# Half of the last pooled output projection moved among the first score tiles of an encoder block

## The chip, the cores and the metric

The kernel runs on one core of a Trainium2 chip. The metric is the device time of one execution in microseconds (us), and the median of several executions counts. The engines are PE (TensorE, the matmuls, with PEld for its weight loads), DVE (VectorE), ACT (ScalarE), POOL (GpSimd) and SP (SyncE, which here only issues DMAs).

## What is computed

One layer of a streaming encoder over 2048 tokens of width 1024: a mixer with two branches, a cross attention to 256 memory tokens and a SwiGLU. The change lies where the mixer's two branches meet:

```python
xn = rmsnorm(h, g_mix[l])
z = jnp.einsum('bsd,dc->bsc', xn, w_in[l])
# q, k, v, p_in, f_logit are column ranges of z; q, k are normalised by head
fox = forgetting_attention(q, k, v, f_logit.transpose(0, 2, 1))   # 8 heads of 64, causal
pool = multiscale_pool(p_in, w_pool[l], pool_scale[l])            # 4 groups of 128 channels
h = h + jnp.einsum('bsc,cd->bsd', jnp.concatenate([fox, pool], axis=-1), w_out[l])
```

`multiscale_pool` takes for group g the trailing mean over 2, 4, 8 or 16 frames less the frame itself, then a 128 x 128 map and a scale per channel. The kernel folds that map into the lower half of `w_out`. The forgetting attention has scores q.k plus a difference of cumulated log gates, a causal mask and a softmax.

## The kernel before

Every float32 operand of a matmul is split into a high and a low part; a product takes three matmuls (`mm3`, lines 69 to 71: high x high, high x low, low x high). Scores take two (line 846).

**Pool stage** (lines 631 to 751). Tokens go in 8 blocks of 256 (two row blocks of 128). Iteration n of a loop of ten projects block n to its pooled channels (`project_p`, tile `zp`), forms the windows on VectorE (`windows`, tile `mixed`), splits `mixed` of block n-1 into `mxh` and `mxl` (`mixed_parts`: a cast on ScalarE, a subtraction on VectorE), and multiplies block n-2 with the folded weights `wop` (`out_pool`). For each row block and each half of 512 columns `out_pool` issues 4 groups x 3 matmuls into a bank `oo`; VectorE adds the bank to the rows of x (`xr`, line 702, "the sum"), and the finished row goes to `h1d` in DRAM (line 703, by GpSimd's queue, for the last block by SP's). In this stage only PE's order is that of the code; a scheduler orders the other engines by their readiness.

**Score stage** (from line 789). Per head and block of 512 rows b there are four rows of 128 (q), and each needs b+1 tiles of up to 512 columns (`score_items`). A tile is two matmuls into one of three banks `sps`, then one reduction on VectorE (line 848), which adds the gates `cb` or, on the diagonal, the masked gates `cm`, and keeps the minimum. `cm` is made by GpSimd (`masked_row`, line 824), three rows ahead, in three small tiles. ScalarE takes the exponential (line 859). 22 score tiles (`LEAD`) go first; then the loop alternates between value steps (`value_items`: transposes `tp`, line 56, their split, the product `acc` with the values, line 922) and score tiles. `later(n, fn)` puts an instruction n steps further into the code. Here PE, DVE, ACT and POOL run in the order of the code.

**Places in SBUF.** A head's `qs`, `kh`, `kl`, `cb` are four tiles of 128 x 2048 in the pool `hpa` (even heads) or `hpb` (odd heads). Head 0 is loaded during the pool stage; `hpb` is opened only behind that stage, and head 1 is loaded into it by SP when head 0 reaches b = 1 (`load_head`, line 619). Before, the `pt` pool holds what the pool stage needs: `xr` (4 row buffers, used in turn, first by the raw weights `wr`), the windows' tiles, `mxh` and `mxl`.

Of the kernel before, what the change touches and what calls it, by code (L numbers as in the profile page):

```python
# [41 lines left out]
def block_kernel(ctx: ExitStack, tc: tile.TileContext, x, xT, memT, cols, rows, w_qkvf, w_p, w_pool, w_out,  # L42
# [9 lines left out]
    def f(ap):  # L52
        return ap.bitcast(F32)
# [141 lines left out]
    with ExitStack() as c0:  # L195
# [167 lines left out]
        with ExitStack() as c1:  # L363
# [129 lines left out]
            def cumulated():  # L493

                HN = H * NT
                cp = lambda n: pt.tile([P, HN], F32, name=n)
                utri, e, mn = cp("utri"), cp("fe"), cp("fmin")
# [9 lines left out]
                yield  # L507
                tots = pt.tile([P, H, NT], F32, name="tots")
                car = pt.tile([P, H, NT], F32, name="car")
                tot = tpp.tile([P, HN], F32, tag="ss", name="tot", bufs=1)  # L510
# [79 lines left out]
            wq_ = opened(xstack, "wo_pool", side="right")  # L590
            pt = opened(xstack, "pt", side="right")
            xt = x_load(1)
            for k in range(NPRE, KD):
# [9 lines left out]
            for g in range(NG):  # L603

                wop_raw.append(pt.tile([P, D], F32, tag="xr", name="wr", bufs=4))
                sp.dma_start(wop_raw[g][:], w_out[FOXW + g * P:FOXW + (g + 1) * P, :])
# [11 lines left out]

    def load_head(h, pl, *after):
        qs, kh, kl = (slab(n, pl, F32R) for n in range(3))  # L620
        cb = slab(3, pl)
        loads = []
        own = slice(h % 2 * DH, (h % 2 + 1) * DH)
        for a in range(2):
            to = slice(a * DH, (a + 1) * DH)
            loads += [(f(qs[to, :]), qkT[0][a][h // 2, own]), (f(kh[to, :]), qkT[1][0][h // 2, own]),
                      (f(kl[to, :]), qkT[1][1][h // 2, own])]
        for to, src in (*loads, (cb[:], cdr[h].partition_broadcast(P))):
            needs(sp.dma_start(to, src), *after)
        return qs, kh, kl, cb  # L630


    with xstack:
# [25 lines left out]
        def windows(b, pT):  # L659
            cur = pT  # L660
            mixed = pt.tile([P, NG, B], F32, tag="mixed", name="mixed")
            for st in range(NG):
                sh = 1 << st
                lead = 2 * sh - 1
                nx = pt.tile([P, NG, HIS + B], F32, tag=f"s{st % 2}", name=f"s{st}")
                dve.tensor_tensor(out=nx[:, st:, lead:], in0=cur[:, st:, lead:],
# [10 lines left out]

        def mixed_parts(mixed):
            mxh = pt.tile([P, NG, B], F32R, tag="mxh", name="mxh", bufs=2)
            mxl = pt.tile([P, NG, B], F32R, tag="mxl", name="mxl", bufs=2)  # L680
            act.copy(mxh[:], mixed[:])
            sub_hi(mxl[:], mixed[:], mxh[:])
            return mxh, mxl
# [3 lines left out]
        def out_pool(b, mxh, mxl):  # L687
            for j in range(2):
                i = 2 * b + j
                ts = slice(j * P, (j + 1) * P)  # L690
                if b < NB - 1:
                    xr = pt.tile([P, D], F32, tag="xr", name="xr", bufs=4)[:]
                    sp.dma_start(xr, x[i * P:(i + 1) * P, :])
                else:
                    xr = x_last[:, j]
                for a in range(2):
                    ps = tpp.tile([P, 512], F32, tag="tp", name="oo", bufs=3)
                    for g in range(NG):
                        mm3(ps[:], (mxh[:, g, ts], mxl[:, g, ts]), (wop[g, a][0][:], wop[g, a][1][:]),
                            g == 0, g == NG - 1)  # L700
                    as_ = slice(a * 512, (a + 1) * 512)
                    summed[:] = [dve.tensor_tensor(out=xr[:, as_], in0=ps[:], in1=xr[:, as_], op=ALU.add)]
                (pool if b < NB - 1 else sp).dma_start(h1d[i][:], xr)

        with in_order():
            mixed, mxs, wop = {}, {}, {}
            for n in range(NB + 2):
# [23 lines left out]
                if n == NB:  # L731
                    lstack.close()
                    hp = opened(hps, "hp")

                    x_last = hp.tile([P, 2, D], F32, tag="v", name="xr", bufs=2)
                    sp.dma_start(x_last[:], x[(NT - 2) * P:, :].rearrange("(j p) c -> p j c", p=P))
                    v0 = load_values(0)
                if n == 2:
                    fold_w_pool()
                if n - 2 >= 0:  # L740
                    out_pool(n - 2, *mxs.pop(n - 2))
                if 0 <= n - 1 < NB:
                    mxs[n - 1] = mixed_parts(mixed.pop(n - 1))
# [22 lines left out]

    FOX = 6
    first_row = []

    TWO, LATER = 3, 7  # L770

    last_parts = []
    hpb = opened(hps, "hpb")
    wof, wq, cats = {}, {}, {}
# [13 lines left out]
    with ExitStack() as c0:  # L788
# [204 lines left out]
        def all_scores():  # L993
            for un in units:
                h, b = un["u"]
                if b == 1 and h + 1 < H:
                    heads[h + 1] = load_head(h + 1, (hpa, hpb)[(h + 1) % 2])
                elif b == 1:
                    load_w_of()
# [12 lines left out]
        def all_values():  # L1012
            for un in units:
                yield from value_items(un)

        def first_fox():
# [13 lines left out]
        with in_order(EN.DVE, EN.Activation, EN.Pool):  # L1030
# [3 lines left out]
            lead, more = 0, True  # L1034
            alone, fox = 0, first_fox()
            while True:
                if more and lead < LEAD:
                    n = next(sg, None)
                    more = n is not None
                    lead += more  # L1040
                else:
                    n = next(vg, None)
# [896 lines left out]
```

## Time and profile before

| | |
|---|---|
| median of 3 executions | 2478.37 us (2477.61 to 2479.3) |
| the profiled execution | 2477.7 us |
| its span, first to last instruction | 2476.0 us |
| PE busy in the span | 2461.1 us (99%) |
| DVE, ACT, POOL busy | 1753.4, 1227.4, 678.7 us |
| pool stage, last matmul issued | 502.27 us after the span's start |

All positions below are microseconds from the span's start. In the trace's rows a matmul of 512 columns is shown with 0.39 us, but its successor may start before it ends; distances between starts are what tells how densely PE issues. "Idle before" an instruction comes in brackets at the end of its row with the one that ended it. In a table of windows each engine has its busy time, with the number of its instructions in brackets.

### The profile page before, as it was taken

The page shows a single profiled execution, that of the slowest core. Times are in us where ns is not written, and L with a number is a line of the kernel's source. Part 1 is how long each engine was busy: PE and PEld are TensorE (multiplying, and loading weights), DVE is VectorE, ACT ScalarE, POOL GpSimd, SP SyncE. Part 2 cuts the span into 40 slices and gives each one's busy share as a digit, 9 for nine tenths or more (in the row PEclk, how much of TensorE's full clock was granted, in tenths as well). Part 3 has the DMA queues.
Part 4 walks back from the last instruction along what each step waited for, and adds up shares of the span by engine and source line. Part 5 has one row for each costly group of instructions (what it writes and reads, how often), then busy time and mean ns, then how long its engine had stood idle before and what let it go on. Part 6 is the DMA issues. An engine that isn't in the chain of part 4 may idle for free.

```text
span 2476.0 us, 37877 instructions
## 1 busy us (share of the span) xinstructions
PE 2461.1 (99%) x13295; PEld 2119.4 (86%) x13295; DVE 1753.4 (71%) x3354; ACT 1227.4 (50%) x2360; POOL 678.7 (27%) x939
## 2 busy tenths in 40 slices
PE   9999999999999999999999999999999999999999
PEld 8999989878888788888888888888888888888887
DVE  7444485489999845456998888867687777775554
ACT  7434441079999845445544444345454333334443
POOL 2233300045555523343133323310002222222000
PEclk9999999999999999999999999999999999999999
DMA  8665566476776543233555554567873233335766
GB/s 296 212 196 168 169 200 175 167 194 155 174 162 157 147 151 107 109 109 128 200 204 196 183 195 167 193 225 254 269 254 107 111 132 115 115 124 179 233 208 209
DMA packets 236991, 436.38 MB, mean 176 GB/s; under 512 B 26416, under 2 KB 124720, under 8 KB 225968
## 3 DMA queue, kind: packets, MB, share of 16 engines
q1 hardware_dynamic: 207536, 339.30, 44.1%
q0 software_dynamic: 29120, 94.39, 10.2%
q8 instruction: 105, 1.72, 0.3%
q14 instruction: 86, 0.70, 0.1%
q10 hardware_dynamic: 144, 0.26, 0.0%
HBM read 295.33 MB, written 133.56 MB: 173 GB/s over the span
## 4 chain that ended last, share of the span: by engine, by line
PE 79%; DMA 3%; DVE 2%; ACT 1%; issue 1%; SPq 0%; POOL 0%; DVEq 0%; ACTq 0%; POOLq 0%
PE bk L69 16%; PE bk L70 15%; PE bk L71 15%; PE acc L922 5%; PE sps L846 5%; PE tp L56 4%; PE mmps L69 3%; PE mmps L70 3%; PE mmps L71 3%; DMA draw<-wt 1%; PE oo L71 1%; PE oo L69 1%; PE oo L70 1%; PE zp L71 1%; PE zp L69 1%; PE zp L70 1%
## 5 line engine op out<-in xcount | busy, mean ns | idle before, releaser
L64 DVE TENSOR_TENSOR ww<-draw,ww 128x512 fp32r<-128x512 f32 x308 | 205.1, 701 | 137.3 <-ACT ww L184 137.0
L184 ACT CAST ww<-draw 128x512 fp32r<-128x512 f32 x308 | 180.7, 620 | 199.8 <-PE bk L71 123.9
L70 PE MATMUL bk<-ww,ww 128*128 128x512 f32 x619 | 240.5, 389 | 1.4 <-DVE ww L64 1.4
L71 PE MATMUL bk<-ww,ww 128*128 128x512 f32 x619 | 240.2, 388 | 0.0
L69 PE MATMUL bk<-ww,ww 128*128 128x512 f32 x619 | 240.2, 388 | 0.0
L64 DVE TENSOR_TENSOR pl<-tp,ph 128x512 fp32r<-128x512 f32 (+3 forms) x298 | 177.0, 596 | 10.3 <-ACT ph L955 10.1
L69 PE MATMUL zps<-wh,xhi 128*128 128x384 f32 (+1 forms) x512 | 174.1, 340 | 0.0
L64 DVE TENSOR_TENSOR ww<-graw,ww 128x512 fp32r<-128x512 f32 x198 | 151.6, 768 | 31.2 <-ACT ww L1166 28.8
L71 PE MATMUL zps<-wh,xl 128*128 128x384 f32 (+1 forms) x512 | 172.0, 336 | 0.0
L70 PE MATMUL zps<-wl,xhi 128*128 128x384 f32 (+1 forms) x512 | 171.9, 336 | 0.0
L1166 ACT CAST ww<-graw 128x512 fp32r<-128x512 f32 x176 | 108.3, 617 | 120.9 <-PE bk L71 112.3
L955 ACT CAST ph<-tp 128x512 fp32r<-128x512 f32 (+3 forms) x298 | 152.5, 529 | 23.5 <-PE tp L56 21.6
L70 PEld LDWEIGHTS bk<-ww,ww 128*128 128x128 f32 x619 | 116.2, 188 | 26.4 <-DVE ww L64 2.6
L69 PE MATMUL bk<-kl,ww 128*128 128x512 f32 x352 | 137.8, 392 | 0.0
L69 PE MATMUL bk<-qs,ww 128*128 128x512 f32 x352 | 137.2, 390 | 0.0
L70 PE MATMUL bk<-kh,ww 128*128 128x512 f32 x352 | 137.2, 390 | 0.0
L71 PE MATMUL bk<-kl,ww 128*128 128x512 f32 x352 | 137.1, 389 | 0.0
L70 PE MATMUL bk<-cb,ww 128*128 128x512 f32 x352 | 137.0, 389 | 0.0
L71 PE MATMUL bk<-qs,ww 128*128 128x512 f32 x352 | 137.0, 389 | 0.0
L69 PEld LDWEIGHTS bk<-ww,ww 128*128 128x128 f32 x619 | 116.2, 188 | 24.0
L71 PEld LDWEIGHTS bk<-ww,ww 128*128 128x128 f32 x619 | 116.2, 188 | 23.9
L846 PE MATMUL sps<-kh,qs 128*128 128x512 f32 (+2 forms) x320 | 124.6, 390 | 0.8 <-DVE mx L848 0.4
(666 smaller groups left out, 7210.5 us busy)
## 6 DMA issues: line engine op xcount, KB each, us to landing
graw<-in_w_gu_dram SPq DMA_DIRECT2D x44, 1024.0 KB, 4.8
draw<-wt SPq DMA_DIRECT2D x88, 256.0 KB, 4.9
draw<-in_w_down_dram SPq DMA_DIRECT2D x66, 256.0 KB, 4.4
xl<-in_xT_dram SPq DMA_DIRECT2D x64, 256.0 KB, 5.9
wdr<-in_w_down_dram SPq DMA_DIRECT2D x44, 256.0 KB, 3.6
wt<-wdr POOLq DMA_DIRECT2D x22, 512.0 KB, 3.1
xrow<-in_x_dram SPq DMA_DIRECT2D x16, 512.0 KB, 5.0
vd<-cb SPq DMA_DIRECT2D x16, 512.0 KB, 3.6
```

What stands on the lines that cost most here:

```text
L56: return pe.transpose(out.bitcast(F32R), src, identr[:])
L64: (eng or dve).tensor_tensor(out=lo, in0=src, in1=f(hi), op=ALU.subtract)
L69: pe.matmul(ps, lhsT=sh, rhs=mh, start=first, stop=False, skip_group_check=goes_on)
L70: pe.matmul(ps, lhsT=sh, rhs=ml, start=False, stop=False, skip_group_check=goes_on)
L71: pe.matmul(ps, lhsT=sl, rhs=mh, start=False, stop=last, skip_group_check=goes_on)
L184: act.copy(hi, raw)
L846: pe.matmul(ps[:, :w], lhsT=qs[:, i * P:(i + 1) * P], rhs=kk[:, cs], start=(a == 0), stop=(a == 1))
L922: pe.matmul(acc[:m, q0 * P:], lhsT=v[:, j, :m], rhs=(pl if low else ph)[:, q0 * P:], start=state["n"] == 1, stop=state["n"] == 2 * nk)
L955: act.copy(ph[:, sl], tp[:, sl])
L1166: w["cast"] = act.copy(quad(hi), v)
```

## The change

The last block's `out_pool` keeps only its left 512 columns. The right 512 columns of its two row blocks (24 matmuls, 2 sums) become a generator `last_pool`, of which one group of three matmuls is issued behind each of the score tiles 4, 6, ... 18 (table `POOLED`). It writes into the banks `acc` that the first value steps use afterwards, and the sums come in two steps later.

For this the operands must outlive the pool stage. `hpb` is opened at n = 8, in place of a new pool `pta` (the `xr` rows, some windows' tiles and the tiles of `cumulated`), which is closed there. `mixed` of the last block is split at once, into `hpb`'s `qs`; the right half of `wop` is copied by eight DMAs of SP, inside SBUF, into `hpb`'s `kh` and `kl`. Rows 12 and 13 of x are loaded and written in halves through the three small tiles that `cm` uses later. The row buffers `xr` are taken in another turn, (i + 2) mod 4. Since `hpb` is in use until score tile 20, the six loads of head 1's `qs`, `kh`, `kl` follow tile 22 and are issued by GpSimd; only its `cb` stays with SP.

```diff
@@ load_head @@
-    def load_head(h, pl, *after):
+    def load_head(h, pl, *after, by=None):
...
-        for to, src in (*loads, (cb[:], cdr[h].partition_broadcast(P))):
+        for to, src in (*(loads if by is None else ()), (cb[:], cdr[h].partition_broadcast(P))):
             needs(sp.dma_start(to, src), *after)
+        if by is not None:
+            by.extend(loads)
@@ out_pool @@
-                if b < NB - 1:
-                    xr = pt.tile([P, D], F32, tag="xr", name="xr", bufs=4)[:]
-                    sp.dma_start(xr, x[i * P:(i + 1) * P, :])
+                if b < NB - 2:
+                    xr_row = pta.tile([P, D], F32, tag=f"xr{(i + 2) % 4}", name="xr", bufs=1)[:]
+                    sp.dma_start(xr_row, x[i * P:(i + 1) * P, :])
+                    xr = [xr_row[:, :512], xr_row[:, 512:]]
+                elif b == NB - 2:
+                    xr = [hp.tile([P, 512], F32, tag="cm", name="xr", bufs=3)[:] for _ in range(2)]
+                    for a in range(2):
+                        sp.dma_start(xr[a], x[i * P:(i + 1) * P, a * 512:(a + 1) * 512])
                 else:
-                    xr = x_last[:, j]
-                for a in range(2):
+                    xr = [x_last[:, j, :512]]
+                for a in range(len(xr)):
...
-                (pool if b < NB - 1 else sp).dma_start(h1d[i][:], xr)
+                    if b == NB - 2:
+                        pool.dma_start(h1d[i][:, a * 512:(a + 1) * 512], xr[a])
+                if b < NB - 2:
+                    pool.dma_start(h1d[i][:], xr_row)
@@ the loop of the pool stage, n == NB @@
                     v0 = load_values(0)
+                    ptas.close()
+                    hpb = opened(hps, "hpb")
+                    last_mx = mixed_parts(mixed.pop(n - 1), slab(0, hpb, F32R)[:])
+                    mxs[n - 1] = last_mx
+                    late_w = [slab(c, hpb, F32R)[:] for c in (1, 2)]
+                    for c in range(2):
+                        for g in range(NG):
+                            sp.dma_start(f(late_w[c][:, g * 512:(g + 1) * 512]), f(wop[g, 1][c][:]))
...
-                if 0 <= n - 1 < NB:
+                if 0 <= n - 1 < NB - 1:
                     mxs[n - 1] = mixed_parts(mixed.pop(n - 1))
@@ the score stage @@
+    POOLED = (4, 6, 8, 10, 12, 14, 16, 18, 20)
...
-                if b == 1 and h + 1 < H:
+                if b == 1 and 0 < h and h + 1 < H:
                     heads[h + 1] = load_head(h + 1, (hpa, hpb)[(h + 1) % 2])
...
+        def last_pool():
+
+            for j in range(2):
+                ps = aps.tile([P, 512], F32, tag="acc", name="oo", bufs=2)
+                ts = slice(j * P, (j + 1) * P)
+                for g in range(NG):
+                    mm3(ps[:], tuple(t_[:, g, ts] for t_ in last_mx), tuple(t_[:, g * 512:(g + 1) * 512] for t_ in late_w),
+                        g == 0, g == NG - 1)
+                    yield
+
+                def summed_(j=j, ps=ps):
+                    xr = x_last[:, j]
+                    dve.tensor_tensor(out=xr[:, 512:], in0=ps[:], in1=xr[:, 512:], op=ALU.add)
+                    sp.dma_start(h1d[NT - 2 + j][:], xr)
+
+                later(2, summed_)
...
                     lead += more
+                    scored += 1
+                    if scored in POOLED:
+                        next(lastp, None)
+                    if scored == POOLED[-1] + 2:
+                        own = []
+                        heads[1] = load_head(1, hpb, by=own)
+                        for m, a_ in enumerate(own):
+                            later(m + 1, lambda a_=a_: pool.dma_start(*a_))
```

On PE, at the first score tiles (`sps`, operands `qs`, `kh`, `kl` of head 0), before the change:

```order
L846 MATMUL sps<-kh,qs 128x384
L846 MATMUL sps<-kl,qs 128x384
L846 MATMUL sps<-kh,qs 128x512
L846 MATMUL sps<-kl,qs 128x512
L846 MATMUL sps<-kh,qs 128x512
```

and after it, where `oo` is the moved product and its `kh`, `kl`, `qs` are `hpb`'s:

```order
L868 MATMUL sps<-kh,qs 128x384
L868 MATMUL sps<-kl,qs 128x384
L868 MATMUL sps<-kh,qs 128x512
L868 MATMUL sps<-kl,qs 128x512
L69 MATMUL oo<-kh,qs 128x512
L70 MATMUL oo<-kl,qs 128x512
L71 MATMUL oo<-kh,qs 128x512
L868 MATMUL sps<-kh,qs 128x512
```

Three matmuls of the pooled projection now stand between the fourth and the fifth score tile, and so on to tile 18.

On GpSimd, from the last rows of the pool stage on (`h1d` is a finished row, `cm` a mask), before:

```order
L703 DMA h1d_121<-xr 128x1024
L824 AFFINE_SELECT cm<-cb 128x128
L824 AFFINE_SELECT cm<-cb 128x256
L824 AFFINE_SELECT cm<-cb 128x384
L831 MEMSET l 128x8
L703 DMA h1d_122<-xr 128x1024
```

and after it:

```order
L715 DMA h1d_124<-xr 128x512 x2
L715 DMA h1d_125<-xr 128x512
L846 AFFINE_SELECT cm<-cb 128x128
L846 AFFINE_SELECT cm<-cb 128x256
L715 DMA h1d_125<-xr 128x512
L846 AFFINE_SELECT cm<-cb 128x384
```

The first three masks have moved behind row 12 and among the halves of row 13. Further on, at score tile 22, GpSimd has after the change:

```order
L846 AFFINE_SELECT cm<-cb 128x256
L1088 DMA qs<-qkT0h 64x2048
L895 TENSOR_TENSOR li<-l 128x4
L1088 DMA kh<-qkT1h 64x2048
L1088 DMA kl<-qkT1l 64x2048
L1088 DMA qs<-qkT0l 64x2048
L1088 DMA kh<-qkT1h 64x2048
L1088 DMA kl<-qkT1l 64x2048
L846 AFFINE_SELECT cm<-cb 128x384
```

Head 1's six loads are new there, between two masks of head 0's last rows.

## Rows read from the trace of the kernel before

**Rows 1.** The page: table of engines (busy us, instructions) and granted clock by slice.
```profile
PE 2461.1 (99%) x13295; PEld 2119.4 (86%) x13295; DVE 1753.4 (71%) x3354; ACT 1227.4 (50%) x2360; POOL 678.7 (27%) x939
...
PEclk9999999999999999999999999999999999999999
```

**Rows 2.** Timeline of PE: start, duration, instruction, idle before it, releaser.
```profile
497.06 0.39 PE L69 MATMUL oo<-wop00h,mxh 128*128 128x512 f32 x1
...
502.51 0.22 PE L846 MATMUL sps<-kh,qs 128*128 128x128 f32 x1
...
503.45 0.45 PE L846 MATMUL sps<-kh,qs 128*128 128x384 f32 x1 [0.32 <-DVE xr L702]
...
514.26 0.46 PE L56 MATMUL tp<-identr,s0g 128*128 128x128 f32 x4
...
535.36 0.29 PE L846 MATMUL sps<-kh,qs 128*128 128x128 f32 x1
```

**Rows 3.** Windows: length, busy time of PE, PEld, DVE, ACT, POOL, clock, DMA.
```profile
502.50:514.26 11.76, 10.97 (x45) 6.71 (x44) 11.22 (x48) 9.14 (x19) 4.74 (x13) 1.00 0.88 206
...
514.26:520.33 6.07, 5.66 (x37) 4.29 (x36) 6.07 (x26) 5.57 (x16) 1.12 (x4) 1.00 1.02 248
520.33:527.63 7.30, 6.80 (x42) 4.92 (x42) 5.79 (x18) 7.08 (x17) 3.92 (x6) 1.00 0.57 221
527.63:535.36 7.73, 7.73 (x55) 6.54 (x55) 7.28 (x24) 6.97 (x14) 3.68 (x5) 1.00 0.37 88
```

**Rows 4.** Waits from 502 to 560: total us, times, longest.
```profile
PEld sps L846 <- DVE mx L848: 4.0, 13, 0.4
```

**Rows 5.** Timeline of VectorE: sums of rows 12 and 13, the last sum, score tiles.
```profile
483.66 0.69 DVE L702 TENSOR_TENSOR xr<-oo,xr 128x512 f32<-128x512 f32 x1 [0.59 <-PE oo L71]
...
491.82 0.69 DVE L702 TENSOR_TENSOR xr<-oo,xr 128x512 f32<-128x512 f32 x1 [2.03 <-PE oo L71]
...
502.71 0.69 DVE L702 TENSOR_TENSOR xr<-oo,xr 128x512 f32<-128x512 f32 x1 [2.04 <-PE oo L71]
...
504.22 0.56 DVE L848 CUSTOM_DVE_ANT_0 s0g<-sps,cm 128x384 f32<-128x384 f32 x1 [0.27 <-PE sps L846]
...
504.70 0.69 DVE L848 CUSTOM_DVE_ANT_0 s0g<-sps,cm 128x512 f32<-128x512 f32 x1
...
505.31 0.69 DVE L848 CUSTOM_DVE_ANT_0 s1g<-sps,cb 128x512 f32<-128x512 f32 x1
```

**Rows 6.** DMA issues in short windows: count, KB each, us from issue to landing.
```profile
h1d<-xr POOLq DMA_DIRECT2D x1, 512.0 KB, 2.9
...
xr<-in_x_dram SPq DMA_DIRECT2D x2, 512.0 KB, 4.1
...
qs<-qkT0h SPq DMA_DIRECT2D x1, 512.0 KB, 5.1
...
kl<-qkT1l SPq DMA_DIRECT2D x1, 512.0 KB, 14.2
...
v<-vd SPq DMA_DIRECT2D x1, 1024.0 KB, 6.9
```

**Rows 7.** Timelines of SP, ScalarE and PE in the early pool stage.
```profile
353.40 0.38 SPq L156 DMA_DIRECT2D xl<-in_xT_dram  x1
...
358.47 0.62 ACT L165 CAST xhi<-xl 128x512 fp32r<-128x512 f32 x1 [1.49 <-DMA xl<-in_xT_dram]
...
361.63 0.39 PE L69 MATMUL oo<-wop31h,mxh 128*128 128x512 f32 x1
```

**Rows 8.** Timeline of GpSimd: the mask ahead of head 1's first load.
```profile
514.98 0.40 POOL L824 TENSOR_SCALAR_AFFINE_SELECT cm<-cb 128x256 f32<-128x256 f32 x1 [1.59 <-DVE mx L848]
```

**Rows 9.** Groups of GpSimd's instructions: busy us, mean ns of one, idle before.
```profile
L906 POOL DMA_DIRECT2D catT<-fo x28 | 24.0, 858 | 12.1 <-DMA catT<-fo 12.1
```

**Rows 10.** SP's queue: first and last of head 2's six loads.
```profile
538.97 0.54 SPq L629 DMA_DIRECT2D qs<-qkT0h  x1
...
542.11 0.59 SPq L629 DMA_DIRECT2D kl<-qkT1l  x1
```

More of the change, by code (lines that the diff above doesn't have):

```diff
@@ L495, in cumulated @@
                 HN = H * NT
-                cp = lambda n: pt.tile([P, HN], F32, name=n)
+                cp = lambda n: pta.tile([P, HN], F32, name=n)
                 utri, e, mn = cp("utri"), cp("fe"), cp("fmin")
@@ L507, in cumulated @@
                 yield
-                tots = pt.tile([P, H, NT], F32, name="tots")
-                car = pt.tile([P, H, NT], F32, name="car")
+                tots = pta.tile([P, H, NT], F32, name="tots")
+                car = pta.tile([P, H, NT], F32, name="car")
                 tot = tpp.tile([P, HN], F32, tag="ss", name="tot", bufs=1)
@@ L591, in block_kernel @@
             pt = opened(xstack, "pt", side="right")
+            ptas = ExitStack()
+            pta = opened(ptas, "pta", side="right")
             xt = x_load(1)
@@ L603, in block_kernel @@
             for g in range(NG):
-                wop_raw.append(pt.tile([P, D], F32, tag="xr", name="wr", bufs=4))
+                wop_raw.append(pta.tile([P, D], F32, tag=f"xr{g}", name="wr", bufs=1))
                 sp.dma_start(wop_raw[g][:], w_out[FOXW + g * P:FOXW + (g + 1) * P, :])
@@ L664, in windows @@
                 lead = 2 * sh - 1
-                nx = pt.tile([P, NG, HIS + B], F32, tag=f"s{st % 2}", name=f"s{st}")
+                nx = (pt if st % 2 else pta).tile([P, NG, HIS + B], F32, tag=f"s{st % 2}", name=f"s{st}")
                 dve.tensor_tensor(out=nx[:, st:, lead:], in0=cur[:, st:, lead:],
@@ L676, in windows, with mixed_parts @@
             return mixed
[L678 to L682, printed above, removed]
+        def mixed_parts(mixed, place=None):
+            if place is None:
+                mxh = pt.tile([P, NG, B], F32R, tag="mxh", name="mxh", bufs=2)[:]
+                mxl = pt.tile([P, NG, B], F32R, tag="mxl", name="mxl", bufs=2)[:]
+            else:
+                mxh, mxl = (place[:, c * NG * B:(c + 1) * NG * B].rearrange("p (g t) -> p g t", g=NG) for c in range(2))
+            act.copy(mxh, mixed[:])
+            sub_hi(mxl, mixed[:], mxh)
             return mxh, mxl
@@ L700, in out_pool @@
                             g == 0, g == NG - 1)
-                    as_ = slice(a * 512, (a + 1) * 512)
-                    summed[:] = [dve.tensor_tensor(out=xr[:, as_], in0=ps[:], in1=xr[:, as_], op=ALU.add)]
-                (pool if b < NB - 1 else sp).dma_start(h1d[i][:], xr)
+                    summed[:] = [dve.tensor_tensor(out=xr[a], in0=ps[:], in1=xr[a], op=ALU.add)]
+                    if b == NB - 2:
+                        pool.dma_start(h1d[i][:, a * 512:(a + 1) * 512], xr[a])
+                if b < NB - 2:
+                    pool.dma_start(h1d[i][:], xr_row)
         with in_order():
@@ L772, in block_kernel @@
     last_parts = []
-    hpb = opened(hps, "hpb")
     wof, wq, cats = {}, {}, {}
@@ L995, in all_scores @@
                 h, b = un["u"]
-                if b == 1 and h + 1 < H:
+                if b == 1 and 0 < h and h + 1 < H:
                     heads[h + 1] = load_head(h + 1, (hpa, hpb)[(h + 1) % 2])
-                elif b == 1:
+                elif b == 1 and h > 0:
                     load_w_of()
@@ L1034, in block_kernel @@
             lead, more = 0, True
-            alone, fox = 0, first_fox()
+            alone, fox, lastp = 0, first_fox(), last_pool()
+            scored = 0
             while True:
```

## The prediction

> **What bounds the kernel now.** [...] In the last row block of the pool stage the first matmul of 24 starts at 497.06 and the first score matmul follows at 502.51 [rows 2]: 24 matmuls of 512 columns in 5.45 us, 0.227 each. Nothing waits there.
>
> Then come the score tiles. The first 22 stand alone on PE, until the first transpose at 514.26 [rows 2]: 11.75 us. They hold 44 matmuls with 17,920 columns in all (1,280 + 3,328 + 4,352 for the first, second and third block of rows, each done twice); at 0.227 per 512 that is 7.95. So 3.8 us of PE are lost. The windows and the waits say to whom: VectorE is busy for 11.22 of 11.76 us, and PE's weight loads wait for its reductions 13 times, 4.0 us in all [rows 3, 4]. A tile of 512 keeps VectorE from 504.70 to 505.31, 0.61 [rows 5], and PE for 0.45, and PE has three banks to run ahead in. After that VectorE is full for 6.07 us more and ScalarE for 7.08 of 7.30, where PE's idle is 0.41 and 0.50 [rows 3]; from 527.63 PE has none.
>
> **The moved matmuls.** 24 of the last 48 matmuls of the pool stage (right half of the columns, both row blocks) go behind score tiles 4, 6, ... 18, three at a time. The score tiles then start 5.45 sooner, at 497.06. PE has 7.95 + 5.45 = 13.4 us to issue in the 22 tiles, VectorE 11.2 plus two sums of 0.6 each (a row is 0.69 long, and the next begins some 0.08 before its end, as the tiles of 512 do [rows 5]) = 12.4. So PE becomes the longer one, and the two are nearly even. If PE never waited, tile 22 would end 13.4 after 497.06 and 3.8 us would be won, all that was lost. Some waits stay: the 0.32 before tile 3 [rows 2], since no group stands ahead of tile 4, and what two engines with 13.4 and 12.4 us of work and three banks between them lose at unequal tiles and where a sum holds VectorE for 0.6, which I put at 0.5. I take 3.8 - 0.8 = **3.0**, with 1.8 (PE pays both sums in full, a further 1.2) and 3.8 as ends.
>
> Behind tile 22 two things pull apart. The sums add 1.2 us to VectorE just ahead of a stretch where it is full; but ScalarE, which is full after that, has had 1 to 2 us longer for the exponentials of these tiles. From the rows the place can give back at most PE's idle, 0.41 + 0.50 = 0.9, and lose half a sum, 0.6. I take 0, nearest to the even sum of both.
>
> **The operand made sooner.** The split of the last block's mixed columns on ScalarE and VectorE now stands ahead of the last-but-one block's projection. VectorE does only a sum every 2.7 us there (483.66 to 491.82, three steps [rows 5]), and PE reads the operand a whole block later. 0, and its bounds with it.
>
> **Copies and halves on SP's queue.** Eight copies inside SBUF (2 MB) wait for the writes of rows 10 and 11, which GpSimd's queue lands 2.9 us after issue [rows 6]. The load of the second half of row 13 stands behind them on SP and waits for the first write of row 12. From the rows: row 12's first sum ends at 484.35 [rows 5], landed at 487.3, then a load that takes 4.1 at most (twice the size, [rows 6]) is there at 491.4; VectorE wants it at 491.82 [rows 5]. Were it 1 us late, VectorE's sum moves, and PE has a free bank: 0. The score masks now use the three small tiles of rows 12 and 13. The second mask waits for row 13's first write (sum at 489.1, landed by 493.2) and the last write stands behind it on GpSimd, so it lands by 496.6 and the third mask is there at about 497.1. VectorE wants it 5.45 before 504.22 [rows 5], at 498.8. I take 0; at 1 us beyond the cover VectorE and then PE pay 1.
>
> **Early row loads.** On SP the loads of rows 0 and 1 now wait for later weight splits, and those of rows 2 and 3 pass three loads of x. There ScalarE waited 1.49 us, until 358.47, for a load of x issued at 353.40; a weight cast stands behind it, which with VectorE's half of the split is done some 1.9 later (two casts of 0.62 [rows 7], a subtraction of 0.69 like the sums) at 360.4; PE reads that weight from 361.63 and its low part a matmul later, at 361.86 [rows 7]. So 1.5 of cover. SP's block moves about 3 us of transfers later, which then flow without gaps. Ends 0 and 1.5; I take 0, since the last of these loads isn't moved itself.
>
> **Head 1 by GpSimd's queue.** Six loads of 512 KB leave SP and follow tile 22 on GpSimd. Ahead of them there stands the mask that was issued at 514.98 [rows 8]; with 3.0 won that is 512.0. Behind them wait the masks of the last two rows of head 0, wanted some 12 us later. What such loads take: head 2's six, issued on SP from 538.97 to 542.11, land 5.1 (the first) and 14.2 us (the last) after their issue, 17.3 from the first issue to the last byte [rows 6, 10]. That gives 529.3. Head 1's first score matmul is at 535.36 [rows 2], with 3.0 won at 532.4: 3 us of margin, and this is the cover. Into it falls the load of head 1's values on SP, 6.9 us by itself [rows 6]; if all of it went ahead, the keys would come at 536.2, 3.8 too late, and PE pays that in full, because its matmuls are in order. Two queues share, so I take 0 and keep 3.8 as the other end.
>
> GpSimd spends 0.86 us on an issue amid busy VectorE [rows 9]; six make 5.2, inside the 17.3. [...]
>
> **Sum.** 3.0 + 0 = 3.0 us, about 0.12%. The profiled execution took 2477.7 (span 2476.0 and 1.7 around it), 0.7 under the median 2478.37. Its successor: 2474.7; against the median **2475.4**. The ends of the first two terms together: 3.8 + 0.9 = 4.7 won and 1.8 - 0.6 = 1.2 won; with the mask or the early loads at their bad end (1 and 1.5) next to nothing is won.
>
> **Rivals.**
> 1. Nearly all 5.45 comes back: ScalarE's chain, not VectorE's, sets the way to 527, and starts 5.4 sooner. For it: ScalarE is full to 527 [rows 3]. Against: VectorE is full before that and gains only 3. 4.0 to 5.4 won: 2473.0 to 2474.4.
> 2. The change only moves the time: the sums and the late mask hold VectorE, which was the bound, and what PE saves ahead it waits among the tiles. For it: VectorE's 11.22 of 11.76. Against: 1.2 us of sums is less than 5.45 of matmuls. 0 to 1 won: 2477.4 to 2478.4.
> 3. Head 1 lands 1 to 4 us late because values and keys share the DMA engines. For it: 17.3 us for the 3 MB of keys alone [rows 6, 10], 20.4 from 512.0 to 532.4 for keys and values. 0 to 2 won: 2476.4 to 2478.4.
> [...]
>
> **How the numbers follow.** The forecast has 0.55, rival 1 0.20, rival 2 0.08, rival 3 0.12, rival 4 0.05. A measurement of this kernel can tell 0.2%, 5.0 us, from no change. Faster by that needs the upper end of rival 1 (over 4.96 won): 0.07. Slower is most of rival 4: 0.04. Same: 0.89. The range for 8 in 10 takes the forecast's 1.2 to 4.7, rival 1 up to 5.2 and rivals 2 and 3 down to 0.8 won: 2473.2 to 2477.6.
>
> **What would show it.** Right: first score matmul at 497.1, 24 matmuls among the tiles, first transpose at 511.2 to 511.6 (13.4 + 0.8 after 497.06), the first score matmul of head 1 at 532 to 533 without a DMA ahead of it, VectorE and PE both without gaps in the 22 tiles. Wrong: a wait of PE for kh or kl of head 1; GpSimd issues over 1 us; VectorE waiting for the third mask; a wait in the early stage at 361; or ScalarE's exponentials running so far ahead that head 1 starts before 531.

## The result and the profile after

The changed kernel takes 2484.99 us (median of nine executions, 2483.32 to 2488.23); the kernel before, on the same chip, 2477.61 (nine, 2475.07 to 2479.35). The ratio is 1.0031, 95% interval 1.0021 to 1.0041: 7.4 us or 0.3% slower, where 2475.4 was forecast and the range ended at 2477.6. (The forecast was taken from the median of three executions, 2478.37; the nine lie 0.8 lower, which changes nothing here.) The profiled execution took 2483.9, its span is 2482.2. PE's busy time is that of [rows 1] to 0.1 us, so the total hides the loss, and the place has to be found on the timeline. The page's table of engines after the change:

```profile
PE 2461.0 (99%) x13295; PEld 2122.5 (86%) x13295; DVE 1751.9 (71%) x3354; ACT 1228.3 (49%) x2360; POOL 679.5 (27%) x947
```

The timeline of PE (start, duration, instruction, idle before it and what ended it) has the answers to [rows 2]: the first score matmul, the first transpose, head 1's first tile, the first transpose of head 0's last block (`s3g`), and the first transpose of head 1 (`s0g` again).

```profile
496.89 0.22 PE L868 MATMUL sps<-kh,qs 128*128 128x128 f32 x1
...
512.41 0.46 PE L56 MATMUL tp<-identr,s0g 128*128 128x128 f32 x4
...
535.54 0.30 PE L868 MATMUL sps<-kh,qs 128*128 128x128 f32 x1 [1.87 <-DMA kh<-qkT1h]
539.00 0.44 PE L868 MATMUL sps<-kl,qs 128*128 128x128 f32 x1 [3.17 <-DMA kl<-qkT1l]
...
548.12 0.51 PE L56 MATMUL tp<-identr,s3g 128*128 128x128 f32 x4 [1.13 <-DVE pl L64]
...
566.24 0.46 PE L56 MATMUL tp<-identr,s0g 128*128 128x128 f32 x4
```

Before the change the last two are here:

```profile
541.27 0.50 PE L56 MATMUL tp<-identr,s3g 128*128 128x128 f32 x4
...
559.42 0.46 PE L56 MATMUL tp<-identr,s0g 128*128 128x128 f32 x4
```

The start of the scores moved as forecast. Two executions differ by up to 2 us in where the same work stands long before the change, so I count from a mark that all kernels here have ahead of any changed wait: VectorE's first sum of row 11, before and after:

```profile
478.22 0.69 DVE L702 TENSOR_TENSOR xr<-oo,xr 128x512 f32<-128x512 f32 x1 [1.52 <-PE oo L71]
...
477.88 0.69 DVE L713 TENSOR_TENSOR xr<-oo,xr 128x512 f32<-128x512 f32 x1 [1.51 <-PE oo L71]
```

From it the scores start 5.28 sooner (24.29 and 19.01), the first transpose 1.51 sooner, and `s3g` comes **7.19 later** (63.05 and 70.24); head 1's first transpose comes 7.2 later too. So the loss is made between 512 and 548, where head 1 needs its keys. In that stretch the DMA queues say how late they came (issues in short windows: count, KB, us from issue to landing; in this order the last two of head 1's six loads, head 1's values, and `ld`, the 2 KB with the reciprocal row sums of head 0, which come back from DRAM as `lbs`, spread over the partitions):

```profile
kh<-qkT1h POOLq DMA_DIRECT2D x1, 512.0 KB, 19.4
kl<-qkT1l POOLq DMA_DIRECT2D x1, 512.0 KB, 22.3
...
v<-vd SPq DMA_DIRECT2D x1, 1024.0 KB, 16.5
...
ld<-li SPq DMA_DIRECT2D x1, 2.0 KB, 20.3
```

GpSimd's timeline gives the issues of the first and last of the six loads, and what GpSimd does afterwards:

```profile
513.74 0.54 POOL L1088 DMA_DIRECT2D qs<-qkT0h  x1 [0.20 <-PE tp L56]
...
516.54 0.52 POOL L1088 DMA_DIRECT2D kl<-qkT1l  x1
...
532.22 1.30 POOL L64 TENSOR_TENSOR pl<-pf,ph 128x512 fp32r<-128x512 f32 x1
543.19 0.92 POOL L928 DMA_DIRECT2D catT<-fo  x1 [9.67 <-DMA catT<-fo]
...
544.25 0.44 POOL L853 MEMSET l<- 128x8 f32 x1
```

The last `kl`, issued at 516.54, landed at 538.84: 25.1 us from the first issue, where head 2's loads took 17.3 on SP [rows 6, 10]. And there is a second wait, of which the prediction knew nothing. GpSimd stands for 9.67 us in front of its catT DMA, an accumulation that must follow SP's catT DMA; `l` and the masks of head 1 stand behind it. SP could give that DMA out only at 538.87, because it stood in front of `lbs` for the `ld` issued at 517.64 (SP's queue):

```profile
517.64 0.58 SPq L899 DMA_DIRECT2D ld<-li  x1
537.98 0.32 SPq L907 DMA_DIRECT2D lbs<-ld  x1
538.39 0.38 SPq L899 DMA_DIRECT2D ld<-li  x1
538.87 0.48 SPq L926 DMA_DIRECT2D catT<-fo  x1
```

Before, GpSimd is at its catT DMA without waiting:

```profile
535.33 0.93 POOL L906 DMA_DIRECT2D catT<-fo  x1
```

The windows (length, busy time of PE, PEld, DVE, ACT, POOL, granted clock, DMA share, GB/s) show the third part:

```profile
536.50:537.00 0.50, 0.00 (x0) 0.00 (x0) 0.00 (x0) 0.00 (x0) 0.00 (x0) 1.00 0.04 0
537.00:538.00 1.00, 0.00 (x0) 0.00 (x0) 0.00 (x0) 0.00 (x0) 0.00 (x0) 0.52 0.00 0
538.00:540.00 2.00, 0.99 (x6) 1.03 (x7) 0.41 (x4) 0.00 (x1) 0.00 (x0) 0.50 0.29 94
540.00:542.00 2.00, 2.00 (x10) 1.73 (x10) 1.15 (x4) 0.81 (x2) 0.00 (x0) 0.50 0.37 104
542.00:543.50 1.50, 1.50 (x5) 1.12 (x4) 0.46 (x2) 1.49 (x3) 0.31 (x1) 0.50 0.62 16
543.50:545.00 1.50, 1.50 (x9) 1.25 (x9) 0.33 (x1) 0.64 (x2) 1.50 (x4) 0.88 0.72 64
```

PE stands from 533.7 but for one matmul; the granted clock falls to 0.50 at about 537, and is back at 1.00 only at about 543.7. "PE busy 2.00" in these rows is a busy PE at about half speed: its matmuls of 512 columns start 0.43 us apart there (541.98, 542.41, 542.84), and 0.23 apart with the clock at 1.00 (544.36, 544.59, 544.82). The rows show one thing more: the DMA engines have moved everything by 536.5, yet the last `kl` counts as landed only at 538.84. The last 2.3 us of its wait hold no transfer.

So PE's 8.7 us between the first transpose (1.51 ahead) and `s3g` (7.19 behind) come apart, but for 0.2, as 5.0 of waiting for keys (1.87 and 3.17), 1.1 of waiting for `pl` behind GpSimd's stand, and, as an estimate from the granted 0.50, 2.4 for the 4.7 us of work that PE did at half the clock from 539.0 to 543.7.

### The profile page after: what moved, and what is told of

Read it like the earlier page. It is cut to its first block, busy times and chain, and to the rows that moved or that the text cites. A ratio compares the mean times of both kernels' runs of the same rounds, so it can differ in the third digit from the quotient of the medians.

```text
span 2482.2 us, 37913 instructions
## 1 busy us (share of the span) xinstructions
PE 2461.0 (99%) x13295; PEld 2122.5 (86%) x13295; DVE 1751.9 (71%) x3354; ACT 1228.3 (49%) x2360; POOL 679.5 (27%) x947
## 4 chain that ended last, share of the span: by engine, by line
PE 84%; issue 7%; DMA 3%; DVE 3%; ACT 1%; POOL 1%; SPq 0%; POOLq 0%; DVEq 0%; ACTq 0%
PE bk L69 15%; PE bk L70 15%; PE bk L71 15%; PE sps L868 5%; PE acc L944 5%; PE tp L56 5%; PE zps L69 4%; PE zps L71 4%; PE zps L70 4%; PE mmps L69 3%; PE mmps L71 3%; PE mmps L70 3%; DMA draw<-wt 1%; DMA xraw<-hTd 1%; DMA wdr<-in_w_down_dram 0%
## 6 DMA issues: line engine op xcount, KB each, us to landing
wt<-wdr POOLq DMA_DIRECT2D x22, 512.0 KB, 3.1
xrow<-in_x_dram SPq DMA_DIRECT2D x16, 512.0 KB, 5.0
vd<-cb SPq DMA_DIRECT2D x16, 512.0 KB, 3.6
```

## The experiments

Each run below is compared with the kernel before on the same chip, in five rounds. "Stretch" is the time from the mark (row 11's first sum) to `s3g`, less the 63.05 us of the kernel before; "to head 1" is the same for head 1's first transpose, less 81.20. Both show the place itself, with no drift from elsewhere, but each comes from one profiled execution (that of keys_sp was the fastest of its eleven, 2478.98 with a median of 2482.04; add_only's eleven spread from 2478.74 to 2485.13).

| run | edit to the changed kernel | ratio (95%) | stretch | to head 1 |
|---|---|---|---|---|
| the changed kernel | | 1.0031 (1.0021 to 1.0041) | +7.2 | +7.2 |
| late_v | values only when keys have landed | 1.0032 (1.0019 to 1.0044) | +7.1 | +9.4 |
| keys_sp | keys on SP's queue | 1.0018 (1.0010 to 1.0027) | +3.3 | +3.3 |
| v_behind | values behind keys on GpSimd's queue | 1.0018 (1.0009 to 1.0027) | +3.5 | +6.2 |
| halves | keys in twelve loads | 1.0018 (1.0009 to 1.0027) | +4.4 | +4.4 |
| add_only | GpSimd's catT DMA later | 1.0017 (1.0008 to 1.0026) | +4.1 | +4.4 |
| vb_add | v_behind and add_only | 1.0007 (0.9998 to 1.0016) | +0.8 | +1.2 |
| no_load | without head 1's loads | 0.9995 (0.9986 to 1.0003) | -1.4 | -1.4 |
| masks_free | rows 12, 13 out of the masks' tiles | 1.0037 (1.0024 to 1.0051) | +6.5 | +6.4 |
| no_load_mf | no_load and masks_free | 0.9994 (0.9985 to 1.0003) | -2.4 | -2.4 |
| early_keys | moved matmuls denser, keys sooner | 1.0015 (1.0007 to 1.0024) | +3.2 | +3.2 |
| all_five | vb_add, masks_free, keys at tile 19 | 0.9996 (0.9987 to 1.0005) | -1.3 | -1.3 |
| before_pool22 | *kernel before*, keys by GpSimd at tile 22 | 1.0009 (1.0000 to 1.0017) | +1.6 | +1.6 |
| before_pool5 | *kernel before*, keys by GpSimd at tile 5 | 0.9997 (0.9988 to 1.0006) | 0.0 | 0.0 |

**Whose are the 25 us?** Theory: the keys on GpSimd's queue and the values on SP's share the DMA engines. Rivals: GpSimd's queue is slow, or the loads simply begin too late.

```diff
-            sp.dma_start(f(v[:]), vd[h])
+            by(lambda: needs(sp.dma_start(f(v[:]), vd[h]), *key_loads))   # late_v, head 1
+            by(lambda: pool.dma_start(f(v[:]), vd[h]))                    # v_behind, head 1
...
-                            later(m + 1, lambda a_=a_: pool.dma_start(*a_))
+                            later(m + 1, lambda a_=a_: sp.dma_start(*a_)) # keys_sp
```

> The changed kernel, with one edit: head 1's values (1 MB, SP's queue) are given out only when head 1's six loads on GpSimd's queue have landed. Theory 'shared engines' (the six loads and the values' load run beside each other and take each other's bandwidth): the six loads take about 17 to 19 us from the first issue at 513.7 instead of 25.1, the last lands at 531 to 533, head 1's first score at about 533.7 waits under 0.5 us, the half clock behind it is gone, and the time falls by 6 to 8.5 us, to 2477 to 2479 us. Rival 'GpSimd's queue moves data slowly': the six loads still take 23 us or more, the wait stays over 3 us, the time stays within 2 us of 2485. The values then land some 7 us after the keys, at about 540, before their first use at about 557.

> The changed kernel, with head 1's values given to GpSimd's queue behind the six loads instead of SP's. Neither keys nor SP's order of work is then held by the values. Theory 'shared engines' with two chains: the six loads take 18 to 20.5 us from 513.7, land at 532 to 534.5, the wait at head 1's first score is 0 to 1.3; catT's first DMA goes out by 531 to 533 and GpSimd is free by about 537, so VectorE waits under 2 us; 2478 to 2480.5 us. Rival 'GpSimd's queue is slow': the keys still land at 537 or later, 2484.

> The changed kernel, with head 1's six loads given to SP's queue at the same step instead of GpSimd's, where the values' load stands behind them. Theory 'shared engines': one queue takes the loads in turn, so the six land within 17 to 18 us of the first issue, as head 2's did before the change (17.3), at 530 to 532; no wait, 2476 to 2478 us. Rival 'mere lateness' (the loads begin too late behind tile 22, by whatever queue): the wait at head 1's first score stays over 3 us and the time over 2482. Rival 'GpSimd's queue is slow' expects the same as the theory here.

> The kernel before, with head 1's six loads given to GpSimd's queue behind score tile 22 instead of SP's at tile 5, nothing else moved. SP's queue, with nothing to hold it, gives out the values' load some 9 us ahead of them, so the values should be nearly through when the keys begin. Theory 'shared engines': the six loads take 17 to 20 us from about 515.5, land at 533 to 535.5, head 1's first score at 535.4 waits 0 to 1 us, and the time is that of the kernel before, 2477.5 to 2479. Rivals 'GpSimd's queue is slow' and 'mere lateness': they take 23 to 25 us, land at 539 to 541, the wait is 3.5 to 5 us with the half clock behind it, and the time is 2482 to 2486.

> The kernel before, with head 1's six loads on GpSimd's queue from score tile 5, the place that they had on SP. They begin at about 505.5, with cb and the values (2 MB) on SP's queue beside them from about 504. Theory 'shared engines': 22 to 26 us for the six, landed by 528 to 531.5, before the need at 535.4, no wait, and the time of the kernel before within 1 us (2476 to 2478). Rival 'GpSimd's queue costs in itself' (its issues hold up masks): masks late by up to 3 us and 2478 to 2480.

With the values out of the way the six loads took 21.3 us (late_v) and 21.4 (v_behind, the last `kl` landed 18.6 after its issue at 516.97). With the values gone before they began, 19.4 (before_pool22); at their old place, with the values beginning at the same moment but no `lbs` beside them, 21.0 (before_pool5, where 22 to 26 were expected). On SP's queue the last landed at 531.3 (keys_sp), 16.3 after 514.93, though one `kl` had gone out at 511.15. So the values beside them cost about 4 us of the 25.1. What is left above SP's 17.3 is 2.1 with `lbs` (256 KB) beside the loads (before_pool22) and 4.0 in late_v, where the row that the moved sums finish last (512 KB, written by SP at 513.63; in before_pool22 at 503.98) goes out beside them as well. In the changed kernel GpSimd's queue moved its first bytes only at about 515.8, 2.1 us after its first issue, and SP's row and `lbs` until then. Whether GpSimd's queue costs anything beyond those bytes is not shown. It is harmless where there is time: before_pool5 equals the kernel before. In before_pool22, which has no wait for keys, GpSimd already stands 2.56 us for `catT`, and 1.6 us are lost.

The time did not follow the keys, though. In late_v PE waits 1.31 for `kl`, but the wait of SP for the keys held `catT` as well, and VectorE's longest wait in head 1 is now for GpSimd; PE then stands, and its clock is at half from 544 to 554 (waits from 530 to 550: us in total, times, longest):

```profile
DVE s0g L874 <- POOL l L857: 6.6, 1, 6.6
```

In keys_sp GpSimd waits for `lbs` instead:

```profile
POOL fo L923 <- DMA lbs<-ld: 8.3, 1, 8.3
```

My expectations of 2477 to 2479 and 2476 to 2478 were wrong there (2484.28 and 2482.04 were measured); the second wait carries the time as soon as the first is shorter. In v_behind too the loads took longer than the 18 to 20.5 us expected, and VectorE waited 3.7 for GpSimd's masks, not under 2.

**GpSimd's stand.** If it is a chain of its own, freeing the keys alone must leave it, and freeing GpSimd alone must leave the keys' wait.

```diff
-                later(ADDED, lambda: pool.dma_start(cat, fo[DH:], accum_op=ALU.add))
+                later(ADDED + (20 if (h, b) == (0, 0) else 0), lambda: pool.dma_start(...))  # add_only, vb_add
...
+            for n in range(2):                                            # halves
+                cs = slice(n * S // 2, (n + 1) * S // 2)
+                by.extend((to[:, cs], src[:, cs]) for to, src in loads)
```

> The changed kernel, with head 1's six loads on GpSimd's queue cut into twelve, the first 1024 columns of all three operands ahead of the rest; nothing else moved. The first four row blocks of head 1 need only the first half, which should land by about 527 to 529. Theory 'only the keys' wait': the 5 us wait at head 1's first score and the half clock behind it are gone, time 2476 to 2479. Theory 'two chains' (formed from the run with the values held back: GpSimd stands until about 543 in front of its catT DMA, because the 2 KB of ld crawl through the same traffic, and head 1's masks stand behind it): the keys' wait is gone, but VectorE then waits 4 to 6 us for GpSimd's mask or its l, PE for VectorE, and the time is still 2482 to 2485.

> The changed kernel with one edit: GpSimd's catT DMA of head 0's first block 20 steps later in its order; values, keys and the products fo as in the changed kernel. The keys' wait stays (4 to 5.5 us and the half clock behind it), GpSimd's stand in front of catT becomes a shorter one for lbs. If the keys' wait alone carries the loss: 2483.5 to 2485.5, within 1.5 us of the changed kernel. If the two waits add up: 2481 to 2482.5, as far below it as the same edit brought with the values behind the keys (2.7 us).

> The changed kernel with head 1's values behind the keys on GpSimd's queue, and GpSimd's catT DMA of head 0's first block 20 steps later in its order; the products fo stay at their places, so catT's own DMAs on SP stay ahead of head 2's loads. Theory 'two chains': no wait for keys over 1 us, GpSimd's stand in front of catT under 1.5 us, some 2 us of waiting for lbs in front of the second fo left; 2477 to 2479, below the 2480.5 with the values behind alone and not 2484.8 as with both steps later. If it is 2484 again, the place of the second fo was not the reason for that.

halves has no wait for keys and is still 1.0018 (2480.54, between the two ranges). Not only for the reason expected: GpSimd gave out eight of the twelve loads and then stood at each further one until an earlier one had landed (1.58 us here), so `li` came late and PE lost 2.8 us at 527 already.

```profile
523.35 0.51 POOL L1090 DMA_DIRECT2D qs<-qkT0l  x1 [1.58 <-DMA kh<-qkT1h]
```

Then the four corners. add_only has the keys' waits; GpSimd no longer stands for catT in front of head 1's first masks, only behind the first of them for `lbs` (6.35 us), and VectorE waits for none:

```profile
535.46 0.30 PE L868 MATMUL sps<-kh,qs 128*128 128x128 f32 x1 [1.69 <-DMA kh<-qkT1h]
537.74 0.32 PE L868 MATMUL sps<-kl,qs 128*128 128x128 f32 x1 [1.99 <-DMA kl<-qkT1l]
...
544.87 0.50 PE L56 MATMUL tp<-identr,s3g 128*128 128x128 f32 x4
```

v_behind has GpSimd's stand (4.92 us, until 539.47) and almost no wait for keys:

```profile
535.66 0.30 PE L871 MATMUL sps<-kl,qs 128*128 128x128 f32 x1 [0.84 <-DMA kl<-qkT1l]
...
544.37 0.72 PE L56 MATMUL tp<-identr,s3g 128*128 128x128 f32 x4 [1.19 <-DVE pl L64]
```

vb_add has neither; GpSimd stands 2.68 for `lbs`, and VectorE 1.3 for a mask behind it:

```profile
534.79 0.30 PE L871 MATMUL sps<-kl,qs 128*128 128x128 f32 x1 [0.26 <-DMA kl<-qkT1l]
...
541.64 0.51 PE L56 MATMUL tp<-identr,s3g 128*128 128x128 f32 x4 [0.97 <-DVE pl L64]
```

To `s3g` the stretches are +7.2 (both waits), +4.1 (keys), +3.5 (GpSimd) and +0.8 (neither), as if the two waits added up. But v_behind's clock falls only at about 543.9 and is back at 550.7: that loss lies behind its `s3g`, at 544.37. To head 1's first transpose they are +7.2, +4.4, +6.2 and +1.2. There taking GpSimd's stand alone brings 2.8, taking the keys' wait alone 1.0, taking both 6.0: either wait covers part of the other, and each by itself is enough for a loss. The median times lie 7.4, 3.4, 4.1 and 1.5 us above the kernel before; they have the same order at both ends, but put the two single edits closer together (add_only, at 2480.52, also came out below both of its ranges). What each wait costs by itself is therefore not settled. In add_only, too, the last `kl` took 21.0 us instead of 22.3, so some 1.2 of its gain is the keys' own.

Putting GpSimd's steps still later only moved the stand. late_catT and vb_catT also moved the product `fo` of the second block:

```diff
-            later(SCALE, lambda: scale(unit, fo))
+            later(SCALE + (16 if unit["u"] == (0, 1) else 0), lambda: scale(unit, fo))
...
+                later(ADDED + (24 if (h, b) == (0, 0) else 0), lambda: pool.dma_start(...))
```

> The changed kernel, with two steps of head 0's finish later in GpSimd's order: the catT DMA of its first block 24 steps later, the product fo of its second block 16 steps later, so that head 1's masks no longer stand behind them. Keys, values and their queues as in the changed kernel. If the keys' late landing is enough by itself to cost the time, the waits for kh and kl stay at 4.5 to 5.5 us with the half clock behind them, GpSimd's catT wait falls under 3 us, and the time falls by no more than 1.5 us, to 2483.5 to 2485. If GpSimd's standing in front of catT is what costs, the time falls by 4 us or more.

> The two edits together: values behind the six loads on GpSimd's queue, and the two steps of head 0's finish later. Theory 'two chains out of one traffic': with the values behind, the keys' wait is 0 to 1 us (0.8 in the run that had this edit alone), and with the finish later VectorE no longer waits for head 1's masks; PE's waits between 530 and 550 fall from 4.6 us to under 1.5, no half clock; the time is 2476.5 to 2478.5, 2.5 to 4 us below the run with the values behind alone (2480.5). If it stays at 2480 or over, a third cause is there.

Ratios 1.0050 (1.0037 to 1.0062) and 1.0035 (1.0022 to 1.0048): late_catT is slower than the changed kernel, vb_catT no faster, and both expectations were missed. vb_catT is 0.9 us ahead of the kernel before at `s3g`, and PE hardly waits until 559.9. But `fo` came so late that its catT DMA stood behind head 2's six loads on SP, and GpSimd stood 9.2 us for it in front of its own; PE then lost this much at once:

```profile
566.00 0.72 PE L56 MATMUL tp<-identr,s0g 128*128 128x128 f32 x4 [6.09 <-DVE pl L64]
```

The same mechanism, one head later: 3 MB of loads ahead of a small DMA for which GpSimd stands.

**Does the whole loss hang on the 3 MB?** no_load gives head 1 what lies in its place, without the six loads.

```diff
-                        heads[1] = load_head(1, hpb, by=own)
-                        for m, a_ in enumerate(own):
-                            later(m + 1, lambda a_=a_: pool.dma_start(*a_))
+                        heads[1] = (*own1, cb)      # own1: the tiles of last_mx and late_w
```

> The changed kernel without head 1's six loads: head 1 is computed with what lies in their place (the moved product's operands), so its values are not the reference's; all matmuls, masks and the rest are as before. Theory 'all of the loss comes from these 3 MB': no wait at head 1's first score, no stand of GpSimd, ld and lbs land within 5 us, and the moved matmuls' gain shows, 1.7 to 2.7 us against the kernel before: 2473.7 to 2475 where the kernel before has 2476.5. Rival 'part of the loss is the moved matmuls' own, or the copies', halves' and masks'': 2477 or more.

Yes. The timeline of its PE, at the places shown for the changed kernel:

```profile
512.16 0.45 PE L56 MATMUL tp<-identr,s0g 128*128 128x128 f32 x4
...
533.27 0.29 PE L869 MATMUL sps<-kh,qs 128*128 128x128 f32 x1
...
539.16 0.50 PE L56 MATMUL tp<-identr,s3g 128*128 128x128 f32 x4
```

1.4 us are won against the kernel before and kept to head 1's first transpose; the median, 2475.43, is 0.9 lower, which the interval does not tell from no change (just above the theory's range, and below the rival's 2477). From the loads to no loads is 8.6 us of stretch.

**The first tiles.** Of the forecast 3.0 only 1.5 was won in the 22 tiles (15.52 us instead of 14.2). VectorE's timeline names the late mask:

```profile
493.36 0.69 DVE L713 TENSOR_TENSOR xr<-oo,xr 128x512 f32<-128x512 f32 x1 [3.91 <-DMA xr<-in_x_dram]
...
499.84 0.56 DVE L870 CUSTOM_DVE_ANT_0 s0g<-sps,cm 128x384 f32<-128x384 f32 x1 [1.50 <-POOL cm L846]
```

masks_free gives the four halves the place of head 1's `cb`, loaded ahead of the copies:

```diff
-                    xr = [hp.tile([P, 512], F32, tag="cm", name="xr", bufs=3)[:] for _ in range(2)]
+                    xr = half_rows[2 * j:2 * j + 2]    # quarters of slab(3, hpb), loaded where hpb is opened
```

> The changed kernel, with the four halves of rows 12 and 13 in the place of head 1's cb instead of in the masks' three tiles, and loaded ahead of the eight copies; head 1's cb is loaded behind their writes. Theory: the third mask's lateness (made at 499.3, wanted at 498.3) cost 1.2 to 1.5 us of the 22 first tiles; with masks that wait for no write the first transpose comes at 511.0 to 511.4 instead of 512.4. Head 1's wait for its keys stays (3.5 to 5.5 us), since both the loads and the need move forward together; the time is 2483 to 2484.3. Rival: VectorE's reductions set the pace of these tiles anyway; the first transpose stays at 512.2 to 512.6 and the time at 2485 +- 0.7. If the four loads come later than they do now, rows 12 and 13 wait for them, and the pool stage ends later than 497.

> The same without head 1's six loads (head 1's values not the reference's), and with rows 12 and 13 out of the masks' tiles. If the late third mask cost about 1 us of the first tiles, this is 0.7 to 1.2 us below the run without that edit: 2472.8 to 2474.2. If VectorE's pace hides it, the two are equal within 0.4.

The 22 tiles take 14.70 us in both runs, and no_load_mf gains 2.4 in the stretch where no_load gains 1.4. In the whole time the two pairs do not differ beyond their scatter: 2485.12 and 2475.37 are what the rivals expected, not the theory. So the 0.9 us is shown in the trace alone.

**Sooner, and all together.**

```diff
-    POOLED = (4, 6, 8, 10, 12, 14, 16, 18, 20)
+    POOLED = (2, 4, 5, 7, 8, 10, 11, 13, 14)      # early_keys
+    POOLED = (2, 4, 6, 8, 10, 12, 14, 16, 17)     # all_four, all_five
```

> The changed kernel, with the eight groups of moved matmuls behind score tiles 2, 4, 5, 7, 8, 10, 11 and 13 instead of 4 to 18 and head 1's loads from tile 16 instead of 22; the loads should begin at about 508 to 509 instead of 513.7. Theory 'two chains, both made by 4 MB beside each other before 534': the keys take about 25 us again but land at 533 to 534, within 1 us of the need, and ld, lbs and catT end some 4 us sooner than at 543; the denser matmuls cost up to 1 us in the first tiles; 2479 to 2482. Rival 'the moved matmuls themselves cost the 8 us': the time stays at 2484 or over.

> The last with rows 12 and 13 out of the masks' tiles and the moved matmuls behind tiles 2 to 16, head 1's loads from tile 19. Expected 0.5 to 2 us under that one: 2475.5 to 2478; under the kernel before only if GpSimd's wait for lbs is gone too.

early_keys (2479.42, as expected) has no wait for keys; GpSimd's 7.6 us for `lbs` and its catT DMA are left. Earlier sums of edits (halves_vb_mf 1.0023, vb_catT_mf 1.0033, all_four 1.0023, where times between 2475 and 2478.5 were expected) carried GpSimd's stand along in one of the forms above. all_five, where GpSimd still stands 5.7 us for `lbs` and 2.4 for `catT` but PE waits for neither, is 1.3 us ahead in the stretch and level with the kernel before in time: 2476.13 against 2476.30. No version here beats the kernel before by more than the measurement tells.

## Why the prediction was wrong

**The failed step is head 1's load.** It had 512.0 + 17.3 = 529.3 against a need at 532.4. Measured: first issue 513.74, 25.1 us, landed 538.84; the need was at 477.88 + 55.73 = 533.6 (mark plus no_load's distance to head 1's first tile). So the start was 1.7 late, GpSimd's queue with `lbs` and the last row's write beside it cost about 4 and the values about 4, against 1.2 us that the need came later. "Two queues share, so I take 0" was the wrong choice: sharing is the delay, because the values' 1 MB comes out of the same rate (from 517 to 533 all transfers together moved 220 GB/s at a share of 1.01, and without the values beside them the six loads took 21.3 us in late_v). Even the end of 3.8 us of waiting that was kept beside it was passed, since a duration from SP's queue, with neither the values nor those two transfers beside it, stood for GpSimd's. PE waited 5.0, and then came the half clock (2.4, estimated above), which had no term at all. The prediction had named "a wait of PE for kh or kl of head 1" as a sign of being wrong.

**A whole chain was missing.** The prediction asked what waits behind the loads on GpSimd (masks of head 0) and not which small transfers would cross the same 20 us. `ld`, `lbs` and `catT` did, and GpSimd, with head 1's masks behind it, stood at their end. In the changed kernel's trace this shows in only 1.13 us of PE's waiting, because the keys' wait covers the rest. It comes out when the keys are in time: v_behind loses 6.2 us to head 1's first transpose, vb_add, with GpSimd's DMA moved as well, 1.2.

**The moved matmuls** won 1.5, under the end of 1.8. The mechanism was right (scores from 496.89, PE the longer engine; no_load_mf comes to 2.4), the term for the third mask was not: it was forecast for 497.1 and was ready at 499.8, and VectorE waited 1.50 for it. Row 13's second load landed at 493.36 behind the copies, not 491.4, and the first write of row 13, issued at 489.75, landed only at 496.4, not 493.2, with the rest of the copies and head 1's `cb` beside it. "1 us beyond the cover" was the end named for it.

**Terms that held.** Behind tile 22 nothing is won or lost: no_load is 1.42 ahead of the kernel before at the first transpose and 1.41 at head 1's first tile. The operand made sooner costs nothing: VectorE's sums keep their step of 2.72 us (480.60, 483.32, 486.04). The early row loads cost nothing: ScalarE's cast and PE's matmul of [rows 7] stand at 358.08 and 361.29.

**The rivals.** Rival 4's 0.05, and with it most of the 0.04 for slower, stood for loads that GpSimd gives out slowly. No run shows such issues: the six took 0.51 to 0.55 us each in the changed kernel and 0.51 to 0.56 in before_pool22, and without the loads (no_load) the 7.4 us are gone. Rival 3 had the right mechanism for the first wait, and stopped at 4 us late and none of the second wait.

## What to carry to other kernels

When a load is moved, ask not only whether it still lands in time by itself, but what else must cross the DMA engines in its new place, and above all which engine stands in order behind the smallest of those transfers (here SP and, behind it, GpSimd, which stood 9.67 us). Where two queues overlap, charge the sum of their bytes to both (here the values' 1 MB cost the keys about 4 us). A cover of 3 us was no cover for loads of 17.3 us that took 25.1 beside others, and an edit that takes one of two waits should be tried together with the one that takes the other.

## What the runs showed of the hardware

**The keys' loads, to 64 partitions, moved at about half the rate of those to 128.** Two windows of the kernel before: head 1's keys (64 partitions each), and then their tail with the gates `cb` and the values (128 partitions each):

```profile
508.00:518.00 10.00, 9.47 (x43) 6.03 (x43) 9.95 (x42) 8.26 (x20) 3.15 (x10) 1.00 1.02 211
518.00:525.00 7.00, 6.37 (x45) 5.10 (x45) 5.70 (x19) 7.00 (x17) 1.37 (x2) 1.00 0.88 319
```

The engines are busy throughout in the first and move 211 GB/s. From 520.6, where the last of the keys had landed (issued at 506.36, 14.2 us), to 522.6 `cb` and the values moved 404 GB/s at a share of 1.05. That the number of partitions makes the difference is not shown: no run here loads the keys to 128 partitions at once.

**A transfer of 2 KB took 20.3 us.** It was `ld`, behind the values on SP's queue with the keys beside it. With the keys on the other queue and only `lbs` (256 KB) ahead on its own, SP, which waits for it, went on 13.5 us after the issue (v_behind, 517.12 to 530.58); with the values ahead and no keys, 5.7 (no_load, 516.91 to 522.57). How a DMA engine divides its time between two queues is not shown.

**The clock fell where PE stood, in more places than one**: to 0.50 at 537 in the changed kernel, in v_behind at about 544 (PE busy for 1.8 of the 4 us ahead), in vb_catT at about 564, and in the first two it was back some 7 us later. In add_only, where PE's two waits were 1.69 and 1.99, it was at half only from about 537.9 to 541.3. In halves PE stood for 2.8 us at 527 and the granted clock stayed at 1.00.
